# Gate gathers of the expert lists issued several items ahead, in front of the V rows

## The chip, the cores and the metric

The kernel runs on one core of one Trainium2 chip. Its time is device microseconds of one execution; three executions before the change gave 2484.81, 2481.37 and 2484.16 us, median 2484.16 us. A further execution was recorded by the profiler. All durations below are from that one.

## The reference

One layer of a diffusion backbone over 256 latent tokens of width 2048: a modulated norm, a joint projection into an mLSTM and a differential attention branch, merging projections, and then an expert retrieval (PEER). The change lies in the last part of the expert retrieval. There every token has 8 heads with 16 chosen experts each out of 16,384; with `idx` the chosen experts and `g` their softmaxed scores,

```python
act = gelu(einsum('td,ted->te', hx, expert_u[ix]))
out = einsum('te,ted->td', g * act, expert_v[ix])
```

and the layer ends in a gated residual and a final RMSNorm.

## The kernel before

The kernel never gathers rows of `expert_u`. It multiplies all 16,384 experts with all 256 tokens (the U stage, until about 2021 us of the span), 256 experts at a time, and writes the activations to a DRAM table `ag_dram`. A row of the table is one expert: 128 activations and 128 routing gates for token tile 0, and as many for token tile 1. The gates were written there earlier.

While U runs, `lists()` sorts the experts that any token uses into blocks of 128 experts and leaves their row numbers in two index tables: `idxV` for rows of `expert_v`, `idxG` for rows of `ag_dram`. The V stage then takes one block after the other: gather 128 rows of `expert_v` (a tile `vraw`, 128x2048 f32, 1.05 MB), gather the same experts' activations and gates (a tile `ag`, the *gates* below), multiply activations with gates (`w`), and multiply on TensorE into eight PSUM accumulators `v` (two token tiles, four column blocks of 512).

There are 65 items of work, in a fixed order `ITEMS`, of four kinds:

- **both** (37): one block whose experts are used by tokens of both tiles. The gates are 128x512 (262 KB). ScalarE and VectorE split `w` into a high and a low half (`l`, lines 1450 and 1451) and each half of `vraw` into `hi` and `lo` (lines 1442 and 1444); TensorE does 24 matmuls of 512 columns (line 1522).
- **one** (14): a block of one token tile. Gates 128x256 (131 KB), 12 matmuls.
- **group** (12): four blocks of 32 tokens each. Four gates of 128x256, four `vraw`; 32 matmuls with 32 columns of weights and no split (weights `w32`, line 1463; matmuls line 1536).
- **dense** (2): the last 256 experts, straight from their activations; no gather.

Items 0 to 2 and 5 are both, 3 and 4 dense, 6 a group. From there on the order repeats in turns of five items, each with one group. Up to item 30 a turn is group, both, one, both, both (6 to 10, 11 to 15, and so on to 26 to 30); from item 35 on group, both, both, one, both (35 to 39, 40 to 44 and so on to 55 to 59); items 31 to 34 are a short turn in between (group, both, one, both). Group 60 is followed by items 61 to 64 and the final norm. A turn holds eight blocks, so eight `vraw` gathers (8.39 MB), and three gathers of 262 KB and five of 131 KB for the gates (1.44 MB).

All gathers are indirect DMAs that GpSimd issues one by one, in the order of the code (`gather`, line 1429, keeps the program order). The `vraw` tiles come in pairs that share a buffer of the pool `gm` (`stage_rows`): four buffers, so eight rows of the list at a time. A pair comes free when the last reader of both of its tiles is done. For a group the readers are its matmuls, for the other kinds the `lo` subtractions. The gates have four buffers for the wide and eight for the narrow kind. `next_item(n)` stages both kinds ahead and makes the weights of item n. Its rule for `vraw` is that a row is issued once its pair's predecessor, eight rows back, lies before item n. Its rule for the gates is `fetch_gates`: those of item n and of the next one.

The order on GpSimd is fixed by the code; on TensorE, ScalarE and VectorE a scheduler orders the instructions at build time by its own estimate, so that moving a gather can also change the order there. All engines execute in that order.

After item 4 there is a branch (`tc.If`, line 1559) for experts that didn't fit the lists; all engines meet there and the body is not taken. Behind it three loads for the final norm are issued (`fin`: line 154 on GpSimd, two more kinds on SyncE), 4.2 MB in all.

Of the kernel before, what the change touches and what calls it, by code (L numbers as in the profile page):

```python
# [19 lines left out]
F32 = mybir.dt.float32  # L20
# [10 lines left out]
P = 128  # L31
# [24 lines left out]
TILES = [(g // 4,) for g in range(8)] + [(0,), (1,), (0, 1)]  # L56
# [3 lines left out]
BOTH, DENSE = 10, 11  # L60


def spread(*groups):
    return [x for _, _, x in sorted(((i + 0.5) / len(g), j, x) for j, g in enumerate(groups) for i, x in enumerate(g))]
# [3 lines left out]
ITEMS = [[(BOTH, i)] for i in range(3)] + [[(DENSE, i)] for i in range(N_LIST, P)] + spread(  # L68
    [[(4 * t + j, i) for j in range(4)] for i in range(6) for t in range(2)],
    [[(BOTH, i)] for i in range(3, CAPS[BOTH])],  # L70
    [[(8 + n % 2, n // 2)] for n in range(11)]) + [[(9, 5)], [(8, 6)], [(9, 6)]]


def build(tc, a, dump=None):
# [27 lines left out]
    def load(src, pool, bufs, queue=nc.sync):  # L102
        r = pool.tile([P, 1024], F32, name="raw", tag="raw", bufs=bufs)
        d = queue.dma_start(r, src)  # L104
        if by_four[0]:
            tc.keep_in_program_order(d)
        return r
# [300 lines left out]
    for k in range(KT):  # L408
# [7 lines left out]
        for kp in range(4):  # L416
            w = load(a["w_mod1"][k, kp], stx, MOD_BUFS)
# [658 lines left out]
    for k in range(KT):  # L1076
        x = rp.tile([P, T], F32, name="xk", tag="xk", bufs=3)
# [329 lines left out]
    n = P - N_LIST + 1  # L1407
# [4 lines left out]
    vst = None  # L1412
# [4 lines left out]
    def stage_rows(kind, i):  # L1417
        if not room:
            two = gm.tile([P, 2, D], F32, name="vraw", tag="gates", bufs=4)
            room.extend(two[:, j, :] for j in range(2))  # L1420
        raw = room.pop(0)
        if kind == DENSE:
            nc.sync.dma_start(raw, FULL[i * P:(i + 1) * P, :])
        else:
            gather(raw, FULL, idxV, BASE[kind] + i)
        return raw

    def gather(out, src, idx, b):
        tc.keep_in_program_order(nc.gpsimd.indirect_dma_start(  # L1429
            out=out, out_offset=None, in_=src, in_offset=bass.IndirectOffsetOnAxis(ap=idx[:, b:b + 1], axis=0)))  # L1430

    def stage_gates(kind, i):
        if kind == DENSE:
            return i
        n = len(TILES[kind])
        ag = vst.tile([P, 2 * n * P], F32, name="ag", tag=f"ag{n}", bufs=(8, 4)[n - 1])
        gather(ag, (ag_tile, ag_dram)[n - 1], idxG, BASE[kind] + i)
        return {t: ag[:, 2 * j * P:2 * (j + 1) * P] for j, t in enumerate(TILES[kind])}

# [14 lines left out]
    def weights_of(kind, ins):  # L1454
        if kind == DENSE:
            r = halves(act_tail[:, ins - N_LIST, :], T, "d", 2)
            return {t: [x[:, t * P:(t + 1) * P] for x in r] for t in range(2)}
        out = {}
        for t, ag in ins.items():
            if kind < 8:  # L1460
                g = slice(32 * (kind % 4), 32 * (kind % 4) + 32)
                out[t] = vst.tile([P, 32], F32, name="w32", tag="w32", bufs=8)
                nc.vector.tensor_tensor(out[t], ag[:, g], ag[:, P:][:, g], op=OP.mult)
                continue
            w = vst.tile([P, P], F32, name="w", tag="w", bufs=2)
            nc.vector.tensor_tensor(w, ag[:, 0:P], ag[:, P:2 * P], op=OP.mult)
            out[t] = halves(w, P, "l", 5)
        return out
# [4 lines left out]
    staged = [0, 0]  # L1473


    def fetch_gates(n):
        while staged[1] < min(len(ITEMS), n):
            gates_in.append([stage_gates(*b) for b in ITEMS[staged[1]]])
            staged[1] += 1

    def next_item(n):
        if n:
            fetch_gates(n + 2)
        while staged[0] < len(ITEMS) and (FIRST_OF[staged[0] + 1] - 1) // 2 * 2 - 7 < FIRST_OF[n]:
            rows_in.append([stage_rows(*b) for b in ITEMS[staged[0]]])
            staged[0] += 1
        fetch_gates(n + 2)
        return [(raw, weights_of(kind, ins)) for (kind, _), raw, ins in
                zip(ITEMS[n], rows_in.pop(0), gates_in.pop(0))]

# [2 lines left out]
    for i1 in range(0, P, 2):  # L1493
        if i1 == N_LIST:

            drain()
            vst = tc.alloc_tile_pool(name="vst", bufs=1, side="right", reuse_waits="tile")
        pss = u_pair(i1, 1.05)
        if i1 == N_LIST:
            (raw0, ins0), = next_item(0)  # L1500
            hl0 = split(raw0[:, 0:1024])
        act = act_tail if i1 == N_LIST else gm.tile([P, 2, T], F32, name="act", tag="act", bufs=2)
        for e, ps in enumerate(pss):
            nc.vector.reduce_sum(act[:, e], ps.rearrange("p s t -> p t s"), axis=AX.X)
        nc.scalar.activation(act, act, AF.Gelu)
        if i1 < N_LIST:
            rows = ag_dram[i1 * P:(i1 + 2) * P].rearrange("(i p) (t c) -> p i t c", p=P, t=2)
            for t in range(2):
                nc.scalar.dma_start(rows[:, :, t, 0:P], act[:, :, t * P:(t + 1) * P])
# [29 lines left out]
    def v_item(n):  # L1539
        parts = next_item(n)  # L1540
        if len(parts) > 1:
            v_groups(ITEMS[n][0][0] // 4, parts)
        else:
            v_block(n, *parts[0])
# [14 lines left out]
    with tc.If(rest > 0):  # L1559
        with tc.For_i(0, N_LIST, 1) as i:  # L1560
            col_ = av.tile([P, 1], F32, name="ocol", bufs=1)
            nc.sync.dma_start(col_, over_dram[:, bass.ds(i, 1)])
            for t in range(2):
                ag = av.tile([P, 2 * P], F32, name="oag", bufs=1)
                nc.sync.dma_start(ag, ag_dram[bass.ds(i * P, P), 2 * t * P:2 * (t + 1) * P])
                w = av.tile([P, P], F32, name="ow", bufs=1)
# [50 lines left out]

    assert [TILES[x[0][0]] for x in ITEMS[N_LAST:]] == [(1,), (0,), (1,)]
    (r0, i0), (r1, i1), (r2, i2) = [next_item(n)[0] for n in range(N_LAST, N_LAST + 3)]
    for hf_ in range(2):  # L1620
        v_part(split(r1[:, hf_ * 1024:(hf_ + 1) * 1024]), i1[0], 0, hf_, last=True)
# [82 lines left out]
```

## Time and profile before

| | |
|---|---|
| median of 3 executions | 2484.16 us |
| profiled execution, its own time | 2482.36 us |
| its span (first to last instruction) | 2480.6 us |
| busy share of PE / DVE / ACT / POOL | 93% / 62% / 46% / 36% |
| U stage ends, V stage begins | about 2021 us |
| group 11 / 31 / 35 / 60 done on TensorE | 2110.7 / 2246.1 / 2273.9 / 2440.2 us |
| from group 60 to the end of the span | 40.4 us |

Times are microseconds from the start of the span. In a row of the timeline stand the start, the duration, the engine, the line, the instruction with output and inputs, how many of the kind follow each other, and in brackets how long the engine was idle before and what it waited for. A row of the waits has the total, the number and the longest. A row of the windows has, for a stretch, its length, the busy time of each engine with its instructions, the granted TensorE clock, the busy share of the 16 DMA engines, and GB/s.

### The profile page before, as it was taken

The page shows a single profiled execution, that of the slowest core. Times are in us where ns is not written, and L with a number is a line of the kernel's source. Part 1 is how long each engine was busy: PE and PEld are TensorE (multiplying, and loading weights), DVE is VectorE, ACT ScalarE, POOL GpSimd, SP SyncE. Part 2 cuts the span into 40 slices and gives each one's busy share as a digit, 9 for nine tenths or more (in the row PEclk, how much of TensorE's full clock was granted, in tenths as well). Part 3 has the DMA queues.
Part 4 walks back from the last instruction along what each step waited for, and adds up shares of the span by engine and source line. Part 5 has one row for each costly group of instructions (what it writes and reads, how often), then busy time and mean ns, then how long its engine had stood idle before and what let it go on. Part 6 is the DMA issues. An engine that isn't in the chain of part 4 may idle for free. (4 is left out here: it accounts for less than half of the span.)

```text
span 2480.6 us, 38079 instructions
## 1 busy us (share of the span) xinstructions
PE 2304.3 (93%) x14434; PEld 1970.7 (79%) x14434; DVE 1545.8 (62%) x2808; ACT 1139.0 (46%) x1913; POOL 897.0 (36%) x910
## 2 busy tenths in 40 slices
PE   6999999999999999999999899999999988778885
PEld 3679989998898999889888788888889875555553
DVE  3457965669767777564979965875654443434435
ACT  3231321345558444444457666964487432323223
POOL 2132201254633000000355754742266224555543
PEclk9999999999999999999999999999999999889987
DMA  9969846875555888655665577888654677787773
GB/s 382 339 209 324 314 161 213 278 209 155 150 177 131 274 277 277 211 189 173 194 193 169 166 222 207 229 221 242 197 177 157 205 264 296 300 312 291 296 279 146
DMA packets 235898, 571.03 MB, mean 230 GB/s; under 512 B 85138, under 2 KB 118723, under 8 KB 221248
## 3 DMA queue, kind: packets, MB, share of 16 engines
q1 hardware_dynamic: 153744, 338.29, 42.5%
q0 software_dynamic: 47120, 212.72, 24.0%
q10 hardware_dynamic: 34848, 17.57, 2.5%
q8 instruction: 113, 1.85, 0.3%
q14 instruction: 73, 0.60, 0.1%
HBM read 524.33 MB, written 38.93 MB: 227 GB/s over the span
## 5 line engine op out<-in xcount | busy, mean ns | idle before, releaser
L120 ACT CAST hi<-raw 128x1024 fp32r<-128x1024 f32 x528 | 552.5, 1048 | 789.5 <-PE acc L275 248.8
L123 DVE TENSOR_TENSOR lo<-raw,hi 128x1024 fp32r<-128x1024 f32 x465 | 591.6, 1275 | 330.4 <-ACT hi L120 329.5
L80 PE MATMUL s<-h,hi 128*128 128x512 f32 x2048 | 737.7, 402 | 3.3 <-ACT hi L120 3.3
L80 PE MATMUL s<-h,lo 128*128 128x256 f32 x2048 | 578.2, 282 | 18.8 <-DVE lo L123 11.6
L80 PEld LDWEIGHTS s<-h,hi 128*128 128x128 f32 x2048 | 386.7, 189 | 90.4 <-ACT hi L120 4.4
L275 PE MATMUL acc<-hL,hi 128*128 128x256 f32 x2048 | 420.4, 285 | 0.0
L80 PEld LDWEIGHTS s<-h,lo 128*128 128x128 f32 x2048 | 389.0, 190 | 26.9 <-DVE lo L123 17.2
L275 PEld LDWEIGHTS acc<-hL,hi 128*128 128x128 f32 x2048 | 339.4, 192 | 4.3 <-issue 3.9
L1522 PE MATMUL v<-hi,l 128*128 128x512 f32 x704 | 217.3, 422 | 84.1 <-ACT l L1450 82.4
L275 PE MATMUL acc<-hL,lo 128*128 128x256 f32 x1024 | 291.1, 285 | 3.1 <-DVE lo L123 3.1
L123 POOL TENSOR_TENSOR lo<-raw,hi 128x1024 fp32r<-128x1024 f32 x63 | 152.6, 2422 | 270.7 <-ACT hi L120 245.1
L1522 PEld LDWEIGHTS v<-hi,l 128*128 128x128 f32 x704 | 138.5, 201 | 139.2 <-ACT l L1450 88.7
L1442 ACT CAST hi<-vraw 128x1024 fp32r<-128x1024 f32 x106 | 109.9, 1047 | 204.5 <-PE v L1522 155.3
L1444 DVE TENSOR_TENSOR lo<-vraw,hi 128x1024 fp32r<-128x1024 f32 x106 | 129.0, 1224 | 114.4 <-ACT hi L1442 94.1
L275 PEld LDWEIGHTS acc<-hL,lo 128*128 128x128 f32 x1024 | 196.4, 192 | 4.6 <-DVE lo L123 3.7
L104 POOL DMA_DIRECT2D raw<-w_mod x128 | 67.9, 531 | 305.0 <-DVE raw L508 283.4
L508 DVE SCALAR_TENSOR_TENSOR raw<-raw,cr 128x1024 f32<-128x1024 f32 x128 | 154.8, 1219 | 35.2 <-DMA raw<-w_mod 19.5
L1223 POOL TENSOR_SCALAR o<-iota,i1T,gT 128x128 f32<-128x128 f32 x128 | 141.2, 1110 | 90.4 <-PE g L80 48.1
L1429 POOL DMA_INDIRECT vraw<-expert_v,idxV x99 | 104.5, 1056 | 168.2 <-PE v L1536 90.5
L275 PE MATMUL acc<-hC,hi 128*128 128x256 f32 x512 | 134.0, 283 | 0.0
L1429 POOL DMA_INDIRECT ag<-ag_dram,idxG x99 | 107.5, 1086 | 49.3 <-issue 26.3
L1522 PE MATMUL v<-lo,l 128*128 128x512 f32 x352 | 122.4, 429 | 2.8 <-DVE lo L1444 2.8
(406 smaller groups left out, 3889.2 us busy)
## 6 DMA issues: line engine op xcount, KB each, us to landing
raw<-expert_u SPq DMA_DIRECT2D x256, 512.0 KB, 4.2
raw<-w_in SPq DMA_DIRECT2D x176, 512.0 KB, 4.6
raw<-w_mod POOLq DMA_DIRECT2D x128, 512.0 KB
raw<-w_mod SPq DMA_DIRECT2D x64, 512.0 KB, 7.8
raw<-w_out SPq DMA_DIRECT2D x32, 512.0 KB, 3.4
raw<-w_pq SPq DMA_DIRECT2D x32, 512.0 KB, 3.4
ag_dram<-gates SPq DMA_DIRECT2D x32, 512.0 KB, 6.6
ag_dram<-act ACTq DMA_DIRECT2D x126, 128.0 KB, 4.2
```

The costliest lines, as they stand in the source:

```text
L80: tc.keep_in_program_order(mm(*args, **kw))
L104: d = queue.dma_start(r, src)
L120: nc.scalar.copy(h, r)
L123: (nc.vector if shared[0] else nc.gpsimd).tensor_tensor(l, r, h.bitcast(F32), op=OP.subtract)
L275: mm(acc[c][:, g * T:(g + 1) * T], lhsT=hl[sb][:, k2 * 512 + c * P:k2 * 512 + (c + 1) * P], rhs=rhs(sa, g, k), start=first and k2 == 0 and ...
L508: product = nc.vector.scalar_tensor_tensor(r, r, 1.0, cr, op0=OP.mult, op1=OP.mult, accum_out=part[:, h, i:i + 1])
L1223: (nc.gpsimd if i % 2 else nc.vector).tensor_scalar(o2[:, i, 0:width], iota[:, 0:width], cols[:, i:i + 1], factor[:, i:i + 1], op0=OP.is_e ...
L1429: tc.keep_in_program_order(nc.gpsimd.indirect_dma_start(out=out, out_offset=None, in_=src, in_offset=bass.IndirectOffsetOnAxis(ap=idx[:, b ...
L1442: nc.scalar.copy(h, raw)
L1444: nc.vector.tensor_tensor(l, raw, h.bitcast(F32), op=OP.subtract)
L1522: mm(out_acc[t][hf_ * 2 + c], lhsT=ins[sa], rhs=hl[sb][:, c * 512:(c + 1) * 512], start=first and i == 0, stop=last and i == 2, skip_group ...
```

## The change

The limit "gates up to item n+1" is replaced by "gates as long as the items from n on need no more than the buffers there are" (eight narrow, four wide; the numbers of buffers are unchanged). Both calls of `fetch_gates` pass n in place of n+2. The first call stands in front of the rows of V, as before, so the gates that newly fit are issued ahead of the rows that are staged at item n.

```diff
-        ag = vst.tile([P, 2 * n * P], F32, name="ag", tag=f"ag{n}", bufs=(8, 4)[n - 1])
+        ag = vst.tile([P, 2 * n * P], F32, name="ag", tag=f"ag{n}", bufs=AG[n - 1])
...
+    AG = 8, 4
+    USES = [[sum(k != DENSE and len(TILES[k]) == w for k, _ in x) for w in (1, 2)] for x in ITEMS]
+
     def fetch_gates(n):
-        while staged[1] < min(len(ITEMS), n):
+        while staged[1] < len(ITEMS) and all(sum(u[w] for u in USES[n:staged[1] + 1]) <= AG[w] for w in range(2)):
             gates_in.append([stage_gates(*b) for b in ITEMS[staged[1]]])
             staged[1] += 1

     def next_item(n):
         if n:
-            fetch_gates(n + 2)
+            fetch_gates(n)
...
-        fetch_gates(n + 2)
+        fetch_gates(n)
```

No gather is added or removed; the lines behind the change move down by three. What moves, at three places:

On GpSimd before, one turn of the first kind, from the staging of item 17 on. In order: gates of 18, rows of group 21, gates of 19 and 20, rows of 22 and 23, gates of 21 and 22, rows of 24 and 25.

```order
L1429 DMA ag<-ag_dram,idxG 128x256
L1429 DMA vraw<-expert_v,idxV 128x2048 x4
L1429 DMA ag<-ag_dram,idxG 128x512 x2
L1429 DMA vraw<-expert_v,idxV 128x2048 x2
L1429 DMA ag<-ag_dram,idxG 128x256 x4
L1429 DMA ag<-ag_dram,idxG 128x512
L1429 DMA vraw<-expert_v,idxV 128x2048 x2
```

The same turn after the change: gates of 21, 22 and 23, rows of group 21, gates of 24, rows of 22 and 23, gates of 25, rows of 24 and 25.

```order
L1429 DMA ag<-ag_dram,idxG 128x256 x4
L1429 DMA ag<-ag_dram,idxG 128x512
L1429 DMA ag<-ag_dram,idxG 128x256
L1429 DMA vraw<-expert_v,idxV 128x2048 x4
L1429 DMA ag<-ag_dram,idxG 128x512
L1429 DMA vraw<-expert_v,idxV 128x2048 x2
L1429 DMA ag<-ag_dram,idxG 128x512
L1429 DMA vraw<-expert_v,idxV 128x2048 x2
```

The gates of 19 and 20 stood behind the rows of 21; now the gates of 24 and 25 stand there, and those of 19 and 20 a turn earlier. The six gathers in front of the rows of 21 were one.

On GpSimd before, a turn of the second kind, from the staging of item 41 on: a row of 44, gates of 43, rows of group 45 and 46, gates of 44 and 45, rows of 47 and 48, gates of 46 and 47.

```order
L1429 DMA vraw<-expert_v,idxV 128x2048
L1429 DMA ag<-ag_dram,idxG 128x256
L1429 DMA vraw<-expert_v,idxV 128x2048 x5
L1429 DMA ag<-ag_dram,idxG 128x512
L1429 DMA ag<-ag_dram,idxG 128x256 x4
L1429 DMA vraw<-expert_v,idxV 128x2048 x2
L1429 DMA ag<-ag_dram,idxG 128x512 x2
```

The same turn after the change: a row of 44, gates of 47 and 48, rows of 45 and 46, gates of 49, rows of 47 and 48, gates of group 50 and of 51.

```order
L1429 DMA vraw<-expert_v,idxV 128x2048
L1429 DMA ag<-ag_dram,idxG 128x512
L1429 DMA ag<-ag_dram,idxG 128x256
L1429 DMA vraw<-expert_v,idxV 128x2048 x5
L1429 DMA ag<-ag_dram,idxG 128x512
L1429 DMA vraw<-expert_v,idxV 128x2048 x2
L1429 DMA ag<-ag_dram,idxG 128x256 x4
L1429 DMA ag<-ag_dram,idxG 128x512
```

The gates of 44 stood behind the rows of 46; now they have gone out a turn earlier. Between the first row and the other five stand two gathers where one stood.

On ScalarE before, the casts of items 42 to 44, in order: the weights of 42, `hi` of 42 (second half) and 43 (first), the weights of 43, `hi` of 43 (second), of 44 (both) and of 46 (first half), and then the weights of 44.

```order
L1450 CAST l_22471<-w 128x128
L1450 CAST l_22477<-w 128x128
L1442 CAST hi<-vraw 128x1024 x2
L1450 CAST l_22517<-w 128x128
L1442 CAST hi<-vraw 128x1024 x4
L1450 CAST l_22554<-w 128x128
L1450 CAST l_22560<-w 128x128
```

After the change: the weights of 42 and 43, `hi` of 41 and 42, the weights of 44, `hi` of 43, the weights of 46, `hi` of 44.

```order
L1450 CAST l_22487<-w 128x128
L1450 CAST l_22493<-w 128x128
L1450 CAST l_22533<-w 128x128
L1442 CAST hi<-vraw 128x1024 x4
L1450 CAST l_22562<-w 128x128
L1450 CAST l_22568<-w 128x128
L1442 CAST hi<-vraw 128x1024 x2
L1450 CAST l_22642<-w 128x128
L1450 CAST l_22648<-w 128x128
```

The weights of 44 stood behind the first `hi` of 46; now they stand in front of the `hi` of 43. VectorE's order moves in the same way. On TensorE a group of the first kind of turn, which stood among the matmuls of the item before it and of the one behind it, now ends before the item behind it begins; what is summed is the same.

## Prediction

> **What bounds the kernel now.** The change touches the V stage alone. I read the page first, then the waits of this stage, then windows of its turns, then the timeline of one turn of each kind. From 2094 us, when the first turns are over, to 2447 us the waits say:
>
> ```profile
> PE v L1522 <- ACT l L1450: 75.7, 11, 8.3
> DVE w L1466 <- DMA ag<-ag_dram,idxG: 88.7, 26, 6.6
> POOL vraw L1429 <- PE v L1536: 82.5, 11, 10.8
> ```
>
> TensorE stands still 11 times, once a turn, about 7 us each, for split weights (`l`) from ScalarE. VectorE in turn waits for gates. GpSimd waits as often for the matmuls of a group, whose rows' buffers it wants. Is anything full? One whole turn (the first row below) and three stretches inside turns:
>
> ```profile
> 2160.20:2194.40 34.20, 26.58 (x116) 17.56 (x116) 13.75 (x26) 10.11 (x16) 16.86 (x17) 0.90 0.76 290
> 2276.00:2292.00 16.00, 12.07 (x52) 9.44 (x51) 6.62 (x7) 5.44 (x6) 12.65 (x12) 1.00 0.99 409
> 2307.00:2325.00 18.00, 11.52 (x50) 9.02 (x48) 6.62 (x7) 5.59 (x7) 12.62 (x12) 0.87 0.99 403
> 2341.00:2358.00 17.00, 11.91 (x52) 9.33 (x50) 6.53 (x7) 5.55 (x6) 12.84 (x12) 1.00 1.00 408
> ```
>
> TensorE (26.58 of 34.20 us) and the DMA engines (0.76) each have a fifth to a quarter of the turn free, and not at the same time: inside a turn the DMA runs full, at about 407 GB/s, while TensorE runs out of work. Why is seen in a turn of the first kind:
>
> ```profile
> 2176.27 1.92 PE L1536 MATMUL v<-vraw,w 128*32 128x512 f32 x16
> 2178.46 1.07 POOL L1429 DMA_INDIRECT vraw<-expert_v,idxV  x1 [4.97 <-PE v L1536]
> 2184.82 0.95 POOL L1429 DMA_INDIRECT ag<-ag_dram,idxG  x1 [0.31 <-issue]
> 2186.15 0.64 PE L1522 MATMUL v<-hi,l 128*128 128x512 f32 x2
> 2193.76 0.49 DVE L1466 TENSOR_TENSOR w<-ag 128x128 f32<-128x128 f32 x2 [4.64 <-DMA ag<-ag_dram,idxG]
> 2194.43 1.22 PE L1522 MATMUL v<-hi,l 128*128 128x512 f32 x2 [7.65 <-ACT l L1450]
> ```
>
> Group 16 ends at 2178.2. Only then may the four rows of group 21 be issued, and only behind them, by the program order, the gates of item 20. Four rows of 1.05 MB at 407 GB/s take 10.3 us, so gates issued at 2184.82 are multiplied at 2193.76, though TensorE had been free since 2186.8. In a turn of the second kind:
>
> ```profile
> 2300.73 3.64 PE L1536 MATMUL v<-vraw,w 128*32 128x512 f32 x32
> 2304.63 0.94 POOL L1429 DMA_INDIRECT vraw<-expert_v,idxV  x1 [9.16 <-PE v L1536]
> 2312.11 1.20 POOL L1429 DMA_INDIRECT vraw<-expert_v,idxV  x1 [0.31 <-issue]
> 2313.61 0.95 POOL L1429 DMA_INDIRECT ag<-ag_dram,idxG  x1 [0.30 <-issue]
> 2324.84 1.04 ACT L1442 CAST hi<-vraw 128x1024 fp32r<-128x1024 f32 x1 [3.52 <-DMA vraw<-expert_v,idxV]
> 2325.38 0.49 DVE L1466 TENSOR_TENSOR w<-ag 128x128 f32<-128x128 f32 x2 [2.80 <-DMA ag<-ag_dram,idxG]
> 2325.79 0.49 ACT L1450 CAST l<-w 128x128 fp32r<-128x128 f32 x2
> 2326.14 1.22 PE L1522 MATMUL v<-hi,l 128*128 128x512 f32 x2 [7.62 <-ACT l L1450]
> 2327.16 1.05 PE L1522 MATMUL v<-lo,l 128*128 128x512 f32 x2
> 2331.55 0.64 PE L1522 MATMUL v<-lo,l 128*128 128x512 f32 x2
> 2332.02 1.09 PE L1522 MATMUL v<-hi,l 128*128 128x512 f32 x4
> ```
>
> Group 40 ends at 2304.4. A row of 44, one gate, the four rows of 45 and the row of 46 follow; the last is issued at 2312.11 and there at 2324.84. The gates of 44 are queued behind it, and so is their cast on ScalarE, behind the `hi` of 46. TensorE waits for item 44, whose rows have long been there. A stall costs twice: the first five pairs after it start 0.85 to 1.02 us apart (2326.14 to 2327.16 is the longest), later ones 0.47 (2331.55 to 2332.02), which is some 2 us more.
>
> **The change, step by step.**
>
> *Gates early (removed wait).* In both kinds the gates that are late now go out about a turn sooner, in front of those rows. Item 20's, issued 9 us before their use now, are then used some 30 us after issue. So the 7.6 us stall and the 2 us behind it go, in every turn. What is late next?
>
> *TensorE.* A turn is 84 matmuls of 512 columns at half of 0.465 us a pair (pairs start at 2331.55 and 2332.02), 19.5 us; a group of 3.6 us (2300.73); about 0.9 us at the changes between the two: 24.0 us.
>
> *DMA.* 9.83 MB at 407 GB/s: 24.2 us. The longest path goes through a group: it ends, its buffers come free, rows are issued, flow and land. Beside their bytes that takes 3.7 us in the first kind (2178.46 to 2193.76 is 15.3 us for four rows and two gates, 11.6 us of bytes) and 4.4 in the second (2304.63 to 2324.84 is 20.2 us for six rows and a narrow gate, 15.8 of bytes). So for the first kind the four rows behind a group are there after 3.7 + 10.3 = 14 us, and TensorE wants them when four items are done, 19.5 us after that group. For the second kind a row, two gates and five rows need 4.4 + 16.4 = 20.8 us up to the row of 46, which is wanted behind the next group, at 24.0. Both fit, the second with 3 us to spare.
>
> *GpSimd.*
>
> ```profile
> L1429 POOL DMA_INDIRECT ag<-ag_dram,idxG x99 | 107.5, 1086 | 49.3 <-issue 26.3 <-SPq L1559 13.8 <-DMA vraw<-expert_v,idxV 6.5
> ...
> 2405.91 1.27 POOL L1429 DMA_INDIRECT vraw<-expert_v,idxV  x1 [10.76 <-PE v L1536]
> ...
> 2412.47 0.94 POOL L1429 DMA_INDIRECT vraw<-expert_v,idxV  x1 [0.30 <-issue]
> 2413.72 1.13 POOL L1429 DMA_INDIRECT vraw<-expert_v,idxV  x1 [0.30 <-issue]
> 2425.30 0.94 POOL L1429 DMA_INDIRECT vraw<-expert_v,idxV  x1 [1.05 <-DMA vraw<-expert_v,idxV]
> 2427.79 0.95 POOL L1429 DMA_INDIRECT ag<-ag_dram,idxG  x1 [1.55 <-DMA vraw<-expert_v,idxV]
> ```
>
> 16 gathers of 1.09 us with 0.30 between them are 22 us a turn; six gates in a row, 8 us, go while rows flow. A gather also waits for the one eight places before it: the fifteenth since 2405.91 (2427.79) waits for the seventh (2413.72), the fourteenth for the sixth. Eight in flight, so gates in front of rows take rows' places. I see no turn in which this empties the DMA queue, but it is the step that the trace of before shows least.
>
> *Added waits.* A gate now waits for its buffer, that is, for the weights of an item before n, and rows queue behind it on GpSimd. Those weights are made before that item's matmuls, which the rows wait for anyway: 0 us while that order holds; the rival on GpSimd prices its failure.
>
> So a turn lies between 24.2 us (DMA full, nothing lost) and the 33.4 of now. I take 25.5 for the first kind and 26 for the second: near the floor, since both paths have room, and above it by the busy TensorE time that these turns show now less the 2 us of slow restarts (26.58 − 2 = 24.6), and 1 to 1.5 us for the latency of rows at a group's end.
>
> *The start.* Two more stalls:
>
> ```profile
> 2058.97 1.18 PE L1522 MATMUL v<-hi,l 128*128 128x512 f32 x4
> 2060.38 1.64 POOL L1429 DMA_INDIRECT ag<-ag_dram,idxG  x1 [0.30 <-issue]
> 2070.87 10.71 PE L1536 MATMUL v<-vraw,w 128*32 128x512 f32 x32 [6.09 <-DVE w L1463]
> 2093.52 0.73 PE L1522 MATMUL v<-hi,l 128*128 128x512 f32 x2 [3.37 <-ACT l L1450]
> 2108.80 1.92 PE L1536 MATMUL v<-vraw,w 128*32 128x512 f32 x16
> ```
>
> The gates of group 6 are issued behind the branch, at 2060.38; with the change they go out ahead of it. So the 6.1 us go, group 6 takes 3.6 in place of 10.7 us, and 3.4 go at 2093.52. From 2058.97 to the end of group 11 are 108 long matmuls (25.1 us), two groups (7.2) and 1.8 of changes: 34.1 us, until 2093.1. I add 2 us, as the rows of 9 and 10 share the DMA with the 4.2 MB of final-norm loads: 2095.1, for 2110.7 now. Ahead of the branch eleven gates stand in front of six's rows, which then go out some 10 us later but are not wanted before 2064: nothing.
>
> The sum, with these ends of groups:
>
> ```profile
> 2244.16 1.92 PE L1536 MATMUL v<-vraw,w 128*32 128x512 f32 x16
> 2270.29 3.63 PE L1536 MATMUL v<-vraw,w 128*32 128x512 f32 x30
> 2436.58 3.64 PE L1536 MATMUL v<-vraw,w 128*32 128x512 f32 x32
> ```
>
> - up to the end of group 11: 2110.7 − 2095.1 = 15.6 us saved
> - groups 11 to 31, four turns: 135.4 now, 4 x 25.5 = 102 then: 33.4
> - 31 to 35, the short turn: 27.8 now; 60 matmuls, a group and the changes are 18.5 on TensorE, seven rows and their gates (8.5 MB) 20.9 on the DMA; I take 21.5: 6.3
> - 35 to 60, five turns: 166.3 now, 5 x 26 = 130 then: 36.3
> - from group 60 on: 40.4 in both; its last row waits for group 60 as before.
>
> Together 91.6 us off the profiled execution's own 2482.4, which is 2390.8. The median of the runs is 1.8 us above that execution: 2392.6.
>
> One rule speaks against the DMA term. The Trainium skill, "DMA: Bandwidth & Descriptors", section Specifications, limits one core's reading from HBM to about 358 GB/s; by it a turn could not go below 9.83 MB / 358 = 27.5 us, the short one below 23.7, and the sum would come to about 2410. The trace does not agree: it holds 403 to 409 GB/s over 16 to 18 us. I go by the rows.
>
> **Rivals.**
>
> *Rows become the bound (0.20).* Gates no longer wait, but rows do: eight places in flight, two gates between the rows of the second kind. For it: 0.99 to 1.00 DMA share inside turns already, and a margin of 3 us that is worked out, not seen. Against it: the weights' casts no longer stand behind the `hi` of the next turn's row. If the second kind stays at 33.3 us, only 15.6 + 33.4 + 6.3 are saved: 2429. If all turns settle at 29 and the short one at 24: 2424.
>
> *Slower (0.03).* Six gates in a row fill six of eight places on GpSimd, and two rows in flight can't keep the DMA busy. Two rows are 5.2 us of bytes in 9.2 us (with 4 of start and landing), so four of a turn's eight rows at that rate cost 4 x 2.0 = 8 us more than with a full queue. With the 24.2 and 4 us exposed at the group a turn is 36.2, 2.8 us more than now, in nine turns 25 us; less the 15.6 of the start that is 2494. It decides if the DMA share of a turn falls below the 0.72 to 0.76 of now. Against it: 0.99 in the windows above, in which gates and rows are mixed too.
>
> *It does nothing (0.02).* If the stalls were ScalarE's order alone and the gates merely land at the same time, taking them ahead moves nothing: 2484. In the second kind both end within a microsecond (2324.84, 2325.38). But the order moves as well, and the first kind shows gates alone.
>
> **How the numbers follow.** The forecast has 0.75: 2392, by itself from 2376 (every turn at its floor, nothing added at the start) to 2412 (turns at 28). The range of 8 in 10 takes in the rows rival and, below, the 2 us by which runs scatter: 2374 to 2429. About 0.2% is what a measurement of this kernel can tell from no change, 5 us; forecast and rows rival are all faster by more: 0.95 faster, 0.02 the same, 0.03 slower.
>
> **What would show it.** Right: TensorE's waits for `l` in the V stage fall from 76 us to under 20, VectorE's for `ag` likewise; turns of about 26 us with a DMA share above 0.9; group 6 in 3.6 us; GpSimd still waits for groups. Wrong: turns of 29 or more with a wait of ScalarE for `vraw` in front of TensorE's stalls (rows), or a DMA share under 0.8 while GpSimd waits for a DMA (places in flight).

## The result, and the profile after

The changed kernel takes 2419.43 us (median of 4 executions, 2414.69 to 2422.88); the kernel before, run beside it, 2483.28 us (2481.37 to 2484.81). The ratio is 0.9742, with a 95% interval of 0.9722 to 0.9762: 64 us faster. The forecast was 2392, the range 2374 to 2429. The profiled execution took 2422.88 us, with a span of 2421.2.

First the waits of the V stage after the change, 2094 to 2390 us (total, number, longest):

```profile
ACT hi L1442 <- PE v L1525: 111.8, 49, 8.3
DVE lo L1444 <- ACT hi L1442: 98.7, 41, 7.7
...
POOL vraw L1429 <- DVE l L1451: 28.9, 8, 5.6
POOL vraw L1429 <- PE v L1539: 25.7, 10, 10.5
...
ACT hi L1442 <- DMA vraw<-expert_v,idxV: 2.2, 2, 1.7
```

No row of the whole answer begins with PE. The 75.7 us in which TensorE stood still for `l` are gone, and so are VectorE's waits for gates; ScalarE waits for rows only 2.2 us. The large waits now end at TensorE, directly or through another engine. Four turns of the first kind as one window, of the kernel before, and then of the one after, group 11 to group 31 in both (the columns as in the prediction: length, busy PE, PEld, DVE, ACT, POOL, clock, DMA share, GB/s):

```profile
2110.70:2246.10 135.40, 105.75 (x466) 69.92 (x462) 55.32 (x106) 40.57 (x61) 67.50 (x64) 0.90 0.76 295
```

```profile
2101.30:2216.40 115.10, 115.10 (x465) 71.65 (x465) 52.84 (x106) 40.33 (x60) 71.20 (x67) 1.00 0.89 344
```

A turn fell from 33.9 to 28.8 us, and TensorE is busy in all of it at the full clock, while the DMA has a tenth free. But the forecast gave TensorE 24.0 us a turn, and the work is the same. Where the other 4.8 us are, the groups of instructions say; first before, then after:

```profile
L1536 PE MATMUL v<-vraw,w 128*32 128x512 f32 x384 | 60.1, 603 | 6.1 <-DVE w L1463 6.1
```

```profile
L1525 PE MATMUL v<-hi,l 128*128 128x512 f32 x704 | 197.7, 398 | 8.7 <-ACT l L1450 8.6
...
L1539 PE MATMUL v<-vraw,w 128*32 128x512 f32 x384 | 104.0, 596 | 0.0
```

The 384 short matmuls of the twelve groups keep TensorE busy for 104.0 us in place of 60.1, though the mean of one is 596 ns, not longer than the 603 of before: each is recorded as long as before, but fewer of them overlap. The timeline shows it for groups 6 and 26 after the change:

```profile
2065.79 1.04 PE L1539 MATMUL v<-vraw,w 128*32 128x512 f32 x2
2068.82 3.63 PE L1539 MATMUL v<-vraw,w 128*32 128x512 f32 x30
...
2176.62 1.90 PE L1539 MATMUL v<-vraw,w 128*32 128x512 f32 x4
2180.52 7.11 PE L1539 MATMUL v<-vraw,w 128*32 128x512 f32 x28
```

Group 6 has nearly the 3.6 us of the forecast (30 of its matmuls in 3.63, the first two earlier); group 26 takes 1.90 + 7.11 = 9.0, and so do ten others. What differs is the order that the scheduler gave TensorE. The first five instructions of the last group, in the order of the program before (`v_...` is a column block, `w_...` the 32 weight columns of one list; the profile counts each of these instructions as two matmuls):

```
MATMUL v_20575<-vraw,w_23228 32x512
MATMUL v_20575<-vraw,w_23230 32x512
MATMUL v_20575<-vraw,w_23232 32x512
MATMUL v_20575<-vraw,w_23234 32x512
MATMUL v_20576<-vraw,w_23228 32x512
```

and after the change:

```
MATMUL v_20585<-vraw,w_23238 32x512
MATMUL v_20586<-vraw,w_23238 32x512
MATMUL v_20587<-vraw,w_23238 32x512
MATMUL v_20588<-vraw,w_23238 32x512
MATMUL v_20585<-vraw,w_23240 32x512
```

Before, in all groups from 11 on but for the first halves of a few, a column block is finished over the four lists, whose weights stand in four different strips of 32 columns of TensorE's array: *by column*. After the change, in all groups but 6, one list goes over four column blocks before the next begins: *by list* (in four of them the first two lists are half mixed, A A B B A B A B). Group 6 is the other way round in both: by list before (10.71 us), by column after.

Theory: the early gates removed TensorE's stalls as forecast, and the missing 27 us went into the groups, because the scheduler, which now perhaps sees the weights of a group ready early, orders it by list, and that costs 9.0 us in place of 3.6. Rivals: the rows or the eight places hold a turn near 28.8 us, and the slow groups only fill it; or the gain came from the other engines' new order and not from the gates; or, for group 6, the prediction's own reading, a slow restart after a stall.

One thing has to be set aside first: TensorE's first V matmul began at 2028.12 us before and at 2031.28 after, and between 2017.5 and 2032.4 in the runs below, though no edit is ahead of it. So beside the medians I compare the *V span* of each profiled execution, from that matmul to the end of the span: 452.5 us before, 389.9 after.

### The profile page after: what moved, and what is told of

Same layout as the page of the kernel before. It is cut to its first block, busy times and chain, and to the rows that moved or that the text cites. A ratio compares the mean times of both kernels' runs of the same rounds, so it can differ in the third digit from the quotient of the medians.

```text
span 2421.2 us, 38180 instructions
## 1 busy us (share of the span) xinstructions
PE 2326.2 (96%) x14434; PEld 1971.9 (81%) x14434; DVE 1542.8 (64%) x2808; ACT 1140.5 (47%) x1913; POOL 894.1 (37%) x910
## 5 line engine op out<-in xcount | busy, mean ns | idle before, releaser
L80 PE MATMUL s<-h,hi 128*128 128x512 f32 x2048 | 740.4, 403 | 1.0 <-ACT hi L120 1.0
L80 PE MATMUL s<-h,lo 128*128 128x256 f32 x2048 | 579.5, 283 | 20.8 <-POOL lo L123 11.5
L80 PEld LDWEIGHTS s<-h,hi 128*128 128x128 f32 x2048 | 388.2, 190 | 88.7 <-ACT hi L120 1.7
L80 PEld LDWEIGHTS s<-h,lo 128*128 128x128 f32 x2048 | 390.0, 190 | 28.7 <-POOL lo L123 14.2
L123 POOL TENSOR_TENSOR lo<-raw,hi 128x1024 fp32r<-128x1024 f32 x63 | 152.4, 2419 | 275.5 <-ACT hi L120 261.7
L1525 PE MATMUL v<-hi,l 128*128 128x512 f32 x704 | 197.7, 398 | 8.7 <-ACT l L1450 8.6
L1525 PEld LDWEIGHTS v<-hi,l 128*128 128x128 f32 x704 | 132.5, 190 | 49.5 <-issue 10.6
L1507 DVE TENSOR_REDUCE act<-s 128x256 f32<-128x512 f32 x126 | 86.4, 686 | 58.1 <-PE s L80 52.8
L1429 POOL DMA_INDIRECT ag<-ag_dram,idxG x99 | 102.6, 1036 | 47.3 <-issue 26.2
```

Of the source, the lines that this page charges most:

```text
L80: tc.keep_in_program_order(mm(*args, **kw))
L123: (nc.vector if shared[0] else nc.gpsimd).tensor_tensor(l, r, h.bitcast(F32), op=OP.subtract)
L1429: tc.keep_in_program_order(nc.gpsimd.indirect_dma_start(out=out, out_offset=None, in_=src, in_offset=bass.IndirectOffsetOnAxis(ap=idx[:, b ...
L1525: mm(out_acc[t][hf_ * 2 + c], lhsT=ins[sa], rhs=hl[sb][:, c * 512:(c + 1) * 512], start=first and i == 0, stop=last and i == 2, skip_group ...
```

## The experiments

**The group's order, with and without the change.** `mp_` keeps instructions in the order of the code (in the profile they have its line, L80). The edit was made to the changed kernel and to the one before:

```diff
-                mm(out_acc[t][c][32 * j:32 * j + 32, :], lhsT=ins[t], rhs=raw[:, c * 512:(c + 1) * 512],
+                mp_(out_acc[t][c][32 * j:32 * j + 32, :], lhsT=ins[t], rhs=raw[:, c * 512:(c + 1) * 512],
```

> The changed kernel, with the matmuls of every group held in the order of the code: column block by column block, so that consecutive matmuls go to four different lists. Theory (TensorE is the bound after the change, and the scheduler's order of the group's matmuls, list by list, costs 9.0 us a group in place of 3.6): groups take 3.6 us again, 5.4 us less in 11 groups is 59 us, of which the DMA floor of 24.2 us a turn lets some 35 to 55 through: 2365 to 2385 us, TensorE busy in over 95% of a turn and the DMA above 0.95. Rival (rows or places in flight hold the turns at 28.8 us, and the slow groups only fill time that would be idle): 2405 to 2420 us, and TensorE waits for casts of rows.

> The kernel before, with the same fixed order by column block and nothing else. Theory: its groups 11 to 60 take 3.6 us already, only group 6 (10.7 us) was list by list, so about 7 us go there and some part of a microsecond in two more: 2470 to 2480 us, with the eleven waits of TensorE for weights as they were. Rival (the gain of the change came from another order on the engines, not from the gates): most of the 64 us come without the change too, under 2440 us.

The changed kernel by column: 2377.63 us, ratio to before 0.9582 (0.9555 to 0.9610), V span 356.3. The kernel before by column: 2469.68 us, 0.9950 (0.9934 to 0.9967), V span 444.7. The first came as the theory said, the second a third of a microsecond below its bound. The changed kernel by column in the same four turns, two of the second kind, and its waits of TensorE from 2060 to 2340 us:

```profile
2083.08:2185.11 102.03, 97.43 (x465) 67.14 (x464) 52.16 (x104) 40.03 (x61) 74.07 (x64) 1.00 0.97 385
```

```profile
2210.06:2256.65 46.59, 46.59 (x234) 33.38 (x233) 25.36 (x52) 19.56 (x30) 33.93 (x32) 1.00 1.01 407
```

```profile
PE v L80 <- DMA vraw<-expert_v,idxV: 9.5, 9, 1.5
PE v L1525 <- ACT hi L1442: 3.1, 5, 0.6
```

102.03 / 4 = 25.5 us a turn, the forecast's own figure, with the DMA at 0.97; two turns of the second kind in 46.6. TensorE waits a little for rows, at no time for weights. So the DMA didn't hold the turn at 28.8. And with the groups held alike in both kernels the change is worth 2469.68 − 2377.63 = 92.1 us by the medians (88.4 by the V spans). The forecast's sum was 91.6, but group 6's gain is in it, and the kernel before by column has part of that already. That the totals agree so closely is partly chance. Nor did the groups' order bring the gain without the gates: by column alone gives 10 us (8 by the V spans). The order on ScalarE and VectorE was not held in any run. What speaks against it as the cause is the trace of before: in the rows of the prediction, VectorE's products wait for gates until 2193.76 and 2325.38, and no order of the casts could have made those weights sooner.

**The other order, forced.** The two loops swapped, so that every group goes by list, again on both kernels:

```diff
-        for c in range(4):
-            for j, (raw, ins) in enumerate(parts):
+        for j, (raw, ins) in enumerate(parts):
+            for c in range(4):
```

> The changed kernel with every group held list by list (four matmuls of one list in succession). Theory (TensorE is the bound): group 6 from 3.6 to 10.7 us, eleven others from 9.0 to 10.7: 7 + 19 = 26 us more, 2445 us. Rival (rows hold the turns): the matmuls are hidden, 2419 to 2427 us.

> The kernel before with every group held list by list. Theory (the order sets a group's time, and a group's end sets when the next rows and the gates behind them are issued): eleven groups from 3.6 to 10.7 us, all of it on the path: 2484 + 70 to 80 = about 2558 us. Rival, the prediction's reading (group 6 took 10.7 us because TensorE restarted slowly behind a stall, not for its order): groups that don't follow a stall keep 3.6 us, 2480 to 2495 us.

The changed kernel by list: 2415.0 us, 0.9732 (0.9704 to 0.9760), V span 390.9, that is the changed kernel itself to 1 us by the V span, so keeping the order of the code costs nothing by itself. The expected 26 us more did not come, since by list takes 8.86 us a group where no stall precedes it, not the 10.7 that I had read off group 6:

```profile
2172.97 8.86 PE L80 MATMUL v<-vraw,w 128*32 128x512 f32 x32
```

The kernel before has both orders with and without a stall ahead; by list:

```profile
2074.43 10.59 PE L80 MATMUL v<-vraw,w 128*32 128x512 f32 x32 [5.70 <-DVE w L1463]
...
2110.66 8.86 PE L80 MATMUL v<-vraw,w 128*32 128x512 f32 x32
```

and by column:

```profile
2067.71 6.78 PE L80 MATMUL v<-vraw,w 128*32 128x512 f32 x32 [5.88 <-DMA ag<-ag_dram,idxG]
2103.31 3.64 PE L80 MATMUL v<-vraw,w 128*32 128x512 f32 x32
```

So the order costs 8.86 − 3.64 = 5.2 us and the restart 1.7 (by list) to 3.1 us (by column): of group 6's 7.1 us too much, the prediction's restart explains the smaller part. The windows of that stall and of the two halves of the group behind it (by column) show the restart in the granted clock (third column from the end):

```profile
2061.80:2067.70 5.90, 0.03 (x1) 0.00 (x0) 1.42 (x2) 1.04 (x1) 4.47 (x5) 0.73 1.01 409
2067.70:2071.10 3.40, 3.39 (x9) 0.92 (x13) 0.94 (x5) 0.04 (x1) 0.95 (x1) 0.50 1.02 411
2071.10:2074.50 3.40, 3.40 (x29) 1.93 (x21) 0.63 (x3) 0.46 (x2) 0.40 (x1) 0.97 0.99 417
```

The clock is 0.50 for the first 3.4 us after the stall of 5.9 us and 0.97 in the next 3.4. The Trainium skill, "TensorE: Matmul & The Clock Gate", Part 1, states half the clock after an idle window of about 3.4 us and all of it after as long a busy one. The trace agrees.

The kernel before by list took 2477.45 us, 0.9986 (0.9973 to 0.9999): neither 2558 nor a group of 3.6 us. Eleven groups got 5.2 us longer and the time did not. TensorE's waits for `l`, 2094 to 2447 us, by list:

```profile
PE v L1522 <- ACT l L1450: 32.8, 11, 4.0
```

and by column:

```profile
PE v L1522 <- ACT l L1450: 72.8, 10, 8.8
```

The longer groups fill the stalls: 40 us of waiting less, of the 57 us (11 x 5.2) that the groups are longer. The granted clock differs too. The same stretch as a window, by list and then by column:

```profile
2094.00:2447.00 353.00, 319.42 (x1247) 199.83 (x1248) 145.11 (x284) 105.72 (x162) 176.84 (x168) 0.97 0.75 293
2094.00:2447.00 353.00, 276.18 (x1256) 193.50 (x1255) 147.54 (x281) 108.28 (x164) 177.64 (x165) 0.88 0.73 283
```

With stalls of at most 4.0 us in place of 8.8 the mean clock is 0.97 in place of 0.88, so less is lost in restarts; how much of the other 17 us that is was not worked out. My step "a group's end sets when the next rows go out" was too coarse. By list, the pair of rows of the first two lists is done in the middle of the group. GpSimd, by list, in the group from 2144.52 to 2153.38 us:

```profile
2150.16 0.93 POOL L1429 DMA_INDIRECT vraw<-expert_v,idxV  x1 [5.18 <-PE v L80]
2151.40 0.94 POOL L1429 DMA_INDIRECT vraw<-expert_v,idxV  x1 [0.31 <-issue]
2153.65 0.94 POOL L1429 DMA_INDIRECT vraw<-expert_v,idxV  x1 [1.32 <-PE v L80]
```

Two of the four rows go out 3.2 and 2.0 us before the group ends, where by column all four wait for its end. So what an order costs depends on the bound: by list is almost free while TensorE waits for gates, and counts once it doesn't: in the changed kernel a turn of the first kind takes about 28.5 us by list and 25.5 by column, 3 of the 5.2 us.

**Two lists at a time.** The changed kernel, with A B A B ... and then C D C D ...:

```diff
-        for c in range(4):
-            for j, (raw, ins) in enumerate(parts):
+        for c, j in [(c, j + k) for j in (0, 2) for c in range(4) for k in range(2)]:
+            for raw, ins in parts[j:j + 1]:
```

> The changed kernel with the matmuls of a group alternating between two of its lists (A B A B ..., then C D C D ...). Theory (a pass costs 277 ns behind another of the same 32 columns of the array and less when the next goes to other columns): between 3.64 and 8.86 us for a group, by half of 277 a pass about 4.5 us, and 2375 to 2390 us in all, as the DMA floor hides the rest. Rival (what counts is only whether all four strips alternate, or whether weights change): 8 to 9 us a group and 2412 to 2422.

2381.20 us, 0.9600 (0.9580 to 0.9620), V span 356.6:

```profile
2233.34 5.38 PE L80 MATMUL v<-vraw,w 128*32 128x512 f32 x32
```

By list, by two and by four lists a group takes 8.86, 5.38 and 3.64 us, 277, 168 and 114 ns a matmul. In these three regular orders a group is the faster the more strips take turns; with two it is slower than the 4.5 us that I had expected. Whether it is the loading of weights or the matmuls themselves that overlap was not separated. How much a half mixed order is worth stays open: the groups with A A B B A B A B in the changed kernel take 7.11 us for their last 28 matmuls, those wholly by list 7.13. At 5.38 us the rest is hidden by the DMA, as expected: the whole takes what it takes by column.

**How far ahead.** The kernel before, by column, with `fetch_gates(n + 3)` and `fetch_gates(n + 4)` in place of `n + 2` in both calls:

> The kernel before with groups by column block, and the gates taken one item further (the limit of both calls n+3 in place of n+2). In turns of the first kind this leaves item 20's gates behind the rows of group 21 (item 19's now stand in front of them); in turns of the second kind it puts item 44's gates in front of the rows of 45 and 46. Theory (what a stall hangs on is whether that one gate stands before or behind those rows): first kind 32.9 us a turn less at most one gather of 1.3, so 31 to 33; second kind 25 to 27.5. With a V stage like the one of before by column block less 4 x 1.3 and 5 x 6.5 us and some for the short turn: 2415 to 2440 us. Rival (depth in general counts, each further item brings a like share): both kinds of turns fall alike, to 28 to 31.

> As the run with n+3, with n+4: item 20's gates too stand in front of the rows of 21. Theory: both kinds of turns at the DMA floor, 24.5 to 26.5 us, and the whole as the changed kernel with groups by column block, 2370 to 2390 us; going further ahead than this brings nothing. Rival (the full depth of the buffers is needed): 2395 us or more.

With n+3: 2399.22 us, 0.9669 (0.9641 to 0.9698), V span 375.0. The second kind of turn fell to 26.3 to 27.4 us but for the last (32.0), as the theory had it; but the first kind fell too, to 25.3 to 27.0, where I had expected 31 to 33. That both kinds fall alike is what the rival said, though it put them at 28 to 31. The trace of before shows an error in my premise. VectorE and GpSimd in the kernel before:

```profile
2183.57 0.95 POOL L1429 DMA_INDIRECT ag<-ag_dram,idxG  x1 [0.30 <-issue]
...
2194.86 0.48 DVE L1466 TENSOR_TENSOR w<-ag 128x128 f32<-128x128 f32 x2
```

The two products at 2193.76, which the prediction puts to item 20, are those of item 19, whose gates went out at 2183.57; item 20's are at 2194.86. TensorE ran dry 8.6 us after group 16 (2178.2 to 2186.8), which is 36 matmuls, items 17 and 18. With n+3 item 19's gates stand in front of the rows, and item 20 is not wanted for another 24 matmuls:

```profile
2139.06 0.63 PE L1522 MATMUL v<-hi,l 128*128 128x512 f32 x2
2141.16 0.73 PE L1522 MATMUL v<-hi,l 128*128 128x512 f32 x2 [1.47 <-ACT l L1450]
```

1.5 us of stall are left, behind a group that ended at 2125.3: 14 us of work, against gates that again take 15 us from the group's end. So the rule can stand with item 19 in place of item 20. By the times alone the rival's general depth would fit as well; what speaks for the rule is these rows.

With n+4: 2367.43 us, 0.9542 (0.9521 to 0.9562), V span 345.1, the shortest time of all runs and a little under the expected 2370. Three of its turns, from 2115 us on:

```profile
2115.00:2185.20 70.20, 70.19 (x348) 49.75 (x348) 40.31 (x78) 29.80 (x45) 49.63 (x48) 1.00 1.02 419
```

23.4 us a turn, with TensorE and the DMA both full; nothing is left to gain there by order. 9.83 MB in 23.4 us are 420 GB/s. The prediction held a figure of the Trainium skill, "DMA: Bandwidth & Descriptors", section Specifications, against its DMA term: about 358 GB/s for a core, which the page gives as a stack's 716 divided by two cores. It does not hold in this kernel, which runs on one core: the trace is 17% above it.

> Groups by column block, gates one item further than in the run with n+4. Theory (from four items on no stall is left, and each further gate in front of a row only delays that row): between the 2367 of four items and the 2378 of the full depth. Rival (deeper is better as long as the buffers hold it, and the difference of the two is scatter): 2360 to 2367 us or less.

With n+5: 2372.40 us, 0.9570 (0.9540 to 0.9600), V span 344.6. The median lies between the two, as the theory had it, but the intervals of n+4, n+5 and the full depth (0.9582) touch, so that deeper costs something is not settled by the times. The V spans (345.1, 344.6, 356.3, one execution each) and GpSimd's rows point to where it would. At full depth, by column, six gates stand in front of the rows of a group that ended at 2133.58:

```profile
2133.28 0.94 POOL L1429 DMA_INDIRECT ag<-ag_dram,idxG  x1 [0.90 <-DMA vraw<-expert_v,idxV]
2135.77 1.58 POOL L1429 DMA_INDIRECT ag<-ag_dram,idxG  x1 [1.55 <-DMA vraw<-expert_v,idxV]
2137.66 1.24 POOL L1429 DMA_INDIRECT ag<-ag_dram,idxG  x1 [0.30 <-issue]
2139.39 1.96 POOL L1429 DMA_INDIRECT vraw<-expert_v,idxV  x1 [0.49 <-PE v L1525]
```

The gates wait for places in flight, and the first of the group's four rows goes out 5.8 us after the group, not 0.3.

**In front of the rows or behind.** The changed kernel by column, without the first call:

```diff
-        if n:
-            fetch_gates(n)
         while staged[0] < len(ITEMS) and (FIRST_OF[staged[0] + 1] - 1) // 2 * 2 - 7 < FIRST_OF[n]:
```

> The changed kernel with groups by column block, without the first call of the gates' staging, the one in front of the rows: gates go as far ahead as the buffers hold, but always behind the rows that are staged at the same item. Theory (they are several items ahead anyway, so the place against those rows doesn't matter): within 6 us of the changed kernel by column block, 2370 to 2385 us. Rival (the place in front of the rows is what helps): TensorE waits for weights again, over 2395 us.

2394.79 us, 0.9654 (0.9632 to 0.9677), V span 370.4: 17 us slower than with the call (14 by the V spans), so "the place doesn't matter" fell. The time is at the rival's bound, but of what TensorE waits for, weights are the smallest part. TensorE, 2060 to 2340 us:

```profile
PE v L1523 <- ACT hi L1442: 10.6, 5, 2.8
PE v L80 <- DMA vraw<-expert_v,idxV: 5.7, 4, 1.4
PE v L80 <- DVE w L1463: 3.3, 2, 3.0
```

It waits for rows above all (`hi` is cast from them). With the gates behind them, rows go out in longer batches, six in a row with seven gathers of gates between the batches, and a batch can start with a wait for a group's weights:

```profile
2134.35 0.94 POOL L1429 DMA_INDIRECT ag<-ag_dram,idxG  x1 [1.54 <-DMA vraw<-expert_v,idxV]
2137.32 0.94 POOL L1429 DMA_INDIRECT vraw<-expert_v,idxV  x1 [2.03 <-DVE w L1463]
```

Which of the two makes the 17 us was not tried.

**Whose order?** The kernel before with n+4 alone, the scheduler free:

> The kernel before with the gates' limit n+4 in place of n+2 and nothing else; the scheduler is free in the groups again. In its order nearly all groups from 11 on stand list by list (A A A A B B B B ...), as in the changed kernel; group 6 and, with n+3, the first half of the groups still stand column by column. Theory (early weights let the scheduler put a whole list first, and that order, not the depth, costs the rest): groups of about 9 us, turns of 28 to 29 us on a TensorE that doesn't wait, 2405 to 2422 us, like the changed kernel. Rival (the full depth or the place of the gates holds the changed kernel at 28.8 us a turn): 2365 to 2385 us, like four items ahead by column.

2417.78 us, 0.9741 (0.9709 to 0.9773), V span 388.5: the changed kernel's time, 50 us above the same kernel by column (43 by the V spans), with groups like this:

```profile
2092.28 8.86 PE L1536 MATMUL v<-vraw,w 128*32 128x512 f32 x32 [0.39 <-DVE w L1463]
```

So neither the full depth nor the place of the gates holds the changed kernel at 28.8 us a turn; early gates bring the order by list with them. In the program with n+3 and a free scheduler, which was not timed, the first half of the groups still stand by column; with n+4 and at full depth nearly all stand by list. That the scheduler does it because it believes the weights ready earlier is argued, not shown.

## Why the prediction was right, and where it was not

The measured 2419 lies in the range, but by luck: it is outside the 2376 to 2412 that the forecast gave itself, and the range reached higher only to take in the rival of rows, which did not happen. The gain was 64 us of the 92. Of the signs of being right, TensorE's and VectorE's waits went, group 6 took nearly 3.6 us and GpSimd still waited for groups; turns of about 26 us with a DMA share above 0.9 did not come (28.8 and 0.89).

By its own parts, in us, for the profiled executions of the kernel before, the forecast, the changed kernel, and the changed kernel by column:

| part | before | forecast | after | after, by column |
|---|---|---|---|---|
| first V matmul to end of group 11 | 82.6 | 67.0 | 70.0 | 65.6 |
| four turns, 11 to 31 | 135.4 | 102 | 115.1 | 102.0 |
| 31 to 35 | 27.8 | 21.5 | 23.2 | 25.0 |
| five turns, 35 to 60 | 166.3 | 130 | 144.0 | 126.2 |
| from group 60 on | 40.4 | 40.4 | 37.5 | 37.5 |
| V span | 452.5 | 360.9 | 389.9 | 356.3 |

- *Gates early*: right. The stalls went in every turn, group 6's wait and the one at 2093.52 with them, and the restarts behind them.
- *TensorE, "a group of 3.6 us (2300.73) ... 24.0 us"*: the step that failed. It priced the group by a row of before and took its order for given, though the change moves instructions by a scheduler, and the front part said that the order can change. The runs showed 8.86 us for a group by list (9.0 in two pieces) and 3.64 by column. Nine turns at 28.8 in place of 25.5 to 26 are 27 of the 29 us by which the V span missed; the smaller terms nearly cancel.
- *"Group 6 takes 3.6 in place of 10.7 us"*: came nearly true, but 10.7 was put down to the stall alone. It was order by list (5.2) and restart (1.7). The row that priced the danger stood in the prediction and was read as something else: 10.71 us for 32 matmuls beside 3.64.
- *DMA, 24.2 us a turn, and the paths through a group*: right where they could be seen, by column: 25.5 for 25.5, and 25.2 on the mean of the second kind for 26, though these five turns run from 23.3 to 29.3 and the short turn took 25.0 for 21.5, so the close sum is in part errors that cancel. The floor is a little lower still (23.4).
- *Added waits, 0*: right for the changed kernel. GpSimd's new wait (`vraw` behind `l` of VectorE, 28.9 us) did not make TensorE wait. At full depth by column the six gates in a row hold rows back by some 6 us, which is the slower rival's mechanism; its price there is at most the 10 us between 2377.63 and 2367.43, and not settled.
- *Item 20*: the products at 2193.76 are item 19's (see n+3). The 3.7 us of the first kind's path would be 4.3 with one gate less in them; the sum does not depend on it.
- *Rivals*: "all turns settle at 29 ... 2424" meets the measured turn and nearly the time, but for a reason that didn't happen: the DMA was at 0.89, and TensorE never waited for a row between 2094 and 2390 us. A number alone would have confirmed the wrong story.

## What to carry to other kernels

When a wait is removed, price the engine that comes next from its order in the changed program, not from a row of the old one; if a scheduler decides that order, look up which neighbours it gives to short instructions. Matmuls that use a strip of the array belong next to matmuls of other strips, and where a scheduler may break that, fix the order: here it was worth 34 us (V spans) to 42 us (medians) on top of the change, and four items ahead with the order fixed took 114 us off the kernel before. Look-ahead paid up to four items, in front of the rows; what goes further stands in front of rows without a stall to remove, and whether that costs time was not settled.

## What the runs showed of the hardware

- Matmuls with 32 columns of weights overlap more when neighbours use different strips: a group of 32 takes 114 ns a matmul with four strips, 168 with two, 277 with one, while each is recorded as about 600 ns long in all cases (the profile models the ends of matmuls). The Trainium skill, "TensorEngine Tiling (Array Packing)", section Tiling Modes, says that different tiles can load weights and multiply in parallel. The trace agrees, and adds that here the order in the program decides how much they do: 8.86 against 3.64 us for the same 32 matmuls.
- Over 70 us, three whole turns, the gathers moved 419 GB/s on one core with TensorE full beside them (n+4 by column).
